# Attention turns of a hybrid mLSTM/Hyena layer: where the raw values are loaded, where the decay products are issued, and how the last two heads' outputs reach the next product

## The chip, the cores and the metric

One core of a Trainium2 chip runs the whole layer in one launch. The metric is the device time of the launch in microseconds; the number given for a kernel is the median of its runs. One more execution was taken with the hardware profiler, and every row below comes from it. Engines are named as in the profile: PE is TensorE (matmuls), PEld its weight loads, ACT is ScalarE, DVE is VectorE, POOL is GpSimd, SP is the engine whose queue issues most DMAs.

## What is computed

One trunk layer over 512 latent tokens of width 1024 with a context of 256 tokens: a modulated RMSNorm, two token mixers side by side (a bidirectional chunkwise mLSTM with 4 heads of width 256, and a Hyena long convolution), a gated merge of the two, an output projection, and a SwiGLU. Only the mLSTM part and what follows it matter here:

```
s   = einsum(q, k) * exp(logD - m_t)              # first products, times the decays
num = einsum(s, v) + a * einsum(C, q)             # second products
den = sum(s) + a * einsum(n, q)
h   = num / max(|den|, exp(-m_t))                 # per direction; h_f + h_b
hm  = head_norm(h_f + h_b, m_norm_g) * sigmoid(o)
y   = gm * (hm @ w_pm) + gh * (hh @ w_ph)         # hh: the Hyena branch
x   = x + g1 * (y @ w_out)
```

The kernel does it without a scan: for each head and direction it makes the full lower (or upper) triangle of decay factors, the context blocks included, so that one head is six source blocks of 128 tokens (four latent, two context) times four target blocks.

## The kernel before

Every fp32 product is made as three products of rounded halves (`mm3`: high times high, high times low, low times high), so each operand is split first: ACT writes the high half (L211), DVE subtracts for the low half (L212).

Raw data comes from DRAM through a ring of four buffers, tag `wr`. Through it go all weights (L236), the weight rows of the adaptive modulation (`wada`, L344, consumed by a DVE step at L354, one per call of `background`), and q, k and v of each head (L894). A buffer is given out in the order in which the program asks for buffers of the ring, and comes free when both halves of the split are made. Split weights go to `wh` and `wl`, four buffers each. The order of the work on each engine is laid down at compile time by a planner that follows the program's order, moves work marked with a high priority ahead, and keeps `behind()` work behind the last matmul of the latest tile product. Each engine then takes its list strictly in turn.

One head's turn, in the loop at L1336 to L1363:

- `load_head(h + 1)` (L885): q, k and v of the next head: five DMAs into the ring and their splits. q's halves have two buffers each, k's halves two buffers in all, v's halves (`vh`, `vl`) one each, so the split of v waits until the second products of the present head are done.
- `decay(h + 1, d)` (L851) for both directions: per direction four row products of 16 partitions into four of the `psH` banks (L862), one mask product (L864), and nine exponentials on ACT (L868).
- `values(h, 0)` (L930): the second products of direction 0, 54 matmuls over four target blocks; then `late`: `head_out` (L962) of the previous head: eight transposes (L966), gate and store of two tiles to DRAM (`hmd`, L976).
- `beside(h, 0)`: a tile of the Hyena projection `wph` (24 matmuls; in heads 0 to 2 only) and one `background` step.
- `weigh(h + 1)` (L913): the first products, 36 matmuls, each times the decays on DVE (L924). `values(h, 1)`; `halves(h + 1)`: the splits of the weighed decays (tags `dx`, `dy`); `beside(h, 1)`; `head_norm(h)` (L950: per target block statistics on DVE, one power on POOL, L958, one DVE step, L959).

In the last head there is no next head. After `late` it reloads six of the eight output tiles from `hmd` (L1265) and splits them; after the loop come two more `wph` tiles, the last `head_out`, whose two tiles are kept and split in SBUF, and the last `wph` tile. Then `staged_gemms("wpm", hm, ...)` makes the merge, whose `merge` calls `background` from its third tile on.

Of the kernel before, what the change touches and what calls it, by code (L numbers as in the profile page):

```python
# [8 lines left out]
F32 = mybir.dt.float32  # L9
# [10 lines left out]
NH = 4  # L20
# [136 lines left out]
def build(nc, tc, I, out, dbg=None):  # L157
# [18 lines left out]
    PR = [0]  # L176
# [5 lines left out]
    def T(p, shape, dt=F32, tag=None, bufs=None):  # L182
        uid[0] += 1
        p = HOME.get(tag, p)
        bufs = BUFS.get(tag, bufs)
        kw = {} if bufs is None else {"bufs": bufs}
        nm = f"{tag or 't'}_{uid[0]}"
        return p.tile(list(shape), dt, tag=tag or nm, name=nm, **kw)
# [21 lines left out]
    def split(hi, lo, x):  # L210
        act.activation(hi, x, AF.Copy)  # L211
        dve.tensor_sub(lo, x, hi.bitcast(F32))  # L212
# [640 lines left out]
    def decay(h, d):  # L853

        w = parts()
        rr = G["rr"]

        def rows(q, n, masked=False):
            ps = bank()
            g = slice(32 * q, 32 * q + 16)  # L860
            s_ = sel[g, 4 * d + h : 4 * d + h + 1].broadcast_to([16, 128])
            pe.matmul(ps[:, :n], s_, rr[g, :n], start=True, stop=not masked)  # L862
            if masked:
                pe.matmul(ps[:, :n], identr[:], mask[:, d : d + 1].broadcast_to([128, 4, 128]), start=False, stop=True)  # L864
            return ps

        def put(s, b0, n, ps, c0, bias):
            act.activation(  # L868
                piece(w, d, s)[:, b0 : b0 + n], ps[:, c0 : c0 + 128 * n].rearrange("p (a b) -> p a b", a=n), AF.Exp, bias=bias
            )  # L870

        pd = rows(0, 512, True)
        for s in range(4):
            put(s, 0 if d == 0 else PIECE[d][s][1] - 1, 1, pd, 128 * s, G["ad"][:, d, s, h : h + 1])
        pc = rows(1, 512)
        for s in range(2):
            put(4 + s, 0, 4, pc, 0, G["ax"][:, d, s, h : h + 1])
        p1 = rows(2, 384)
        p2 = rows(3, 384)
        o = [0, 1, 2] if d == 0 else [3, 2, 1]  # L880
        for s, ps, c0 in ((o[0], p1, 0), (o[1], p2, 0), (o[2], p2, 256)):
            put(s, 1 if d == 0 else 0, PIECE[d][s][1] - 1, ps, c0, G["ao"][:, d, s, h : h + 1])
        return w

    def load_head(h):  # L885

        kh, kl = (T(PT, [128, 2048], F32R, "K")[:, :1536].rearrange("p (a b) -> p a b", a=2) for _ in range(2))
        qh, ql = T(PT, [128, 2, SEQ], F32R, "uh"), T(PT, [128, 2, SEQ], F32R, "ul")

        def staged(src, n, hi, lo, a=None):  # L890
            t = T(PW, [128, WMAX], F32, "wr")[:, :n]
            if a:
                t = t.rearrange("p (a b) -> p a b", a=a)
            dma(t, src)  # L894
            split(hi, lo, t)

        staged(qd[:, 2 * h : 2 * h + 2], 2 * SEQ, qh[:], ql[:], 2)
        if h == 0:
            fill(next(cf))
        for i in range(2):  # L900
            staged(kd[:, 2 * h + i], SEQ + CTX, kh[:, i], kl[:, i])
        if h == 0:
            fill(next(cf))
        Vh, Vl = T(PM_, [128, 6, NV], F32R, "vh"), T(PM_, [128, 6, NV], F32R, "vl")
        gp.memset(Vh[:, :, 256:257].bitcast(F32), 1.0)
        gp.memset(Vh[:, :, 257:258].bitcast(F32), 0.0)
        gp.memset(Vl[:, :, 256:258].bitcast(F32), 0.0)
        for b, n in ((0, 4), (4, 2)):
            staged(vd[:, h, b : b + n], 256 * n, Vh[:, b : b + n, :256], Vl[:, b : b + n, :256], n)
        return (qh, ql), (kh, kl), (Vh, Vl)  # L910

    def weigh(h, qq, kk, Dm):

# [47 lines left out]
    def head_out(h, hs, keep=False):  # L961
        kept = []  # L962
        pt = [bank(), bank()]
        for t in range(4):
            for i in range(2):
                pe.transpose(pt[i][:, 128 * t : 128 * t + 128], hs[:, t, 128 * i : 128 * i + 128], ident)  # L966
        for i in range(2):
            hg = T(PM_, [128, 512], F32, "s2")
            act.activation(hg[:], pt[i][:], AF.Copy, scale=mngh[:, 2 * h + i : 2 * h + i + 1])
            o = T(PM_, [128, SEQ], F32, "s2")  # L970
            dma(o[:], od[:, 2 * h + i])
            dve.scalar_tensor_tensor(hg[:], o[:], 1.0, hg[:], op0=ALU.add, op1=ALU.mult)
            if keep:
                kept.append(hg)
            else:
                store(hmd[:, 2 * h + i], hg[:])  # L976
        return kept
# [166 lines left out]
    def background():  # L1144
        next(later, None)
# [39 lines left out]
    def fill(n):  # L1185
        for _ in range(n):
            if fills:
                fills.pop(0)()
# [98 lines left out]
            yield  # L1287

    fill(next(cf))
    heads = {0: load_head(0)}  # L1290
    sel = T(PM_, [128, 8], F32R, "sel")
    selr = load(PM_, "sel", [128, 8], "selr")
    act.activation(sel[:], selr[:], AF.Copy)
# [4 lines left out]
    act.activation(identr[:], ident, AF.Copy)  # L1298
    target_rows()

    def start(h):
        L = heads.get(h) or load_head(h)
        return L, [decay(h, d) for d in range(2)]

    def steps(n):
        for _ in range(n):
            background()

    L, Dm = start(0)
    fill(next(cf))  # L1310
    ada_row()
    weigh(0, L[0], L[1], Dm)
# [15 lines left out]
            next(ph)  # L1328
        steps(1)

    def late(_=None):
        if done:
            with behind():
                head_out(*done.pop())

    for h in range(NH):  # L1336
        nxt = start(h + 1) if h + 1 < NH else None
        den = T(PM_, [128, 2, 4], F32, "den", 2)
        hs = T(PM_, [128, 4, 256], F32, "hs", 2)
        values(h, 0, W[0], L[2], den, hs)  # L1340
        late(hs)
        if h == NH - 1:
            sp_ = [T(PT, [128, 2048], F32R, "K") for _ in range(2)]
            parts_ = [[v[:, 512 * j : 512 * j + 512] for j in range(4)] for v in sp_]
            for i, tag in enumerate(("uh", "ul")):
                v = T(PT, [128, 2, SEQ], F32R, tag)
                parts_[i] += [v[:, 0], v[:, 1]]
            its = [iter(v) for v in parts_]
            hm = reload(hmd, lambda: next(its[0]), lambda: next(its[1]), range(6))
        beside(h, 0)  # L1350
        if nxt:
            weigh(h + 1, nxt[0][0], nxt[0][1], nxt[1])
        values(h, 1, W[1], L[2], den, hs)
        if nxt:
            Wn = [halves(nxt[1][d]) for d in range(2)]
        beside(h, 1)
        head_norm(hs)
        done.append((h, hs))
        if nxt:
            L, W = nxt[0], Wn  # L1360
    next(ph)
    next(ph)
    with behind():  # L1363
# [45 lines left out]
    def merge(d, ps):  # L1409
        g = scr()  # L1410
        dma(g[:], gmd[:, 0, d])
        t = scr()
        dma(t[:], y2d[:, d])
        dve.scalar_tensor_tensor(g[:], g[:], 1.0, ps[:], op0=ALU.add, op1=ALU.mult)
        dve.tensor_add(g[:], g[:], t[:])
        y[0].append(big())
        y[1].append(big())
        split(y[0][-1][:], y[1][-1][:], g[:])
        if d > 1:
            background()  # L1420

    staged_gemms("wpm", hm, 3, 6, merge, KT)
    dve.tensor_scalar_mul(g1h[:], modT[:, 2, :, 0], 0.5)
# [146 lines left out]
```

## Time and profile before

| | |
|---|---|
| median of 3 runs | 1233.41 us (1231.26 to 1238.62) |
| the profiled execution's own time | 1238.27 us |
| its span in the trace | 1236.5 us |
| PE busy | 1196.6 us, 97% of the span |
| DVE, ACT, POOL busy | 835.0, 529.4, 68.2 us |
| mean granted clock of TensorE | 0.984 of full |

The span is the traced part of the execution; 1.8 us lie around it. Times in rows are microseconds from the span's start. The attention turns take the stretch from about 613 to 768 us. A busy PE may still be a slow one: the granted clock has two levels, 2.4 GHz (1.00) and 1.2 GHz (0.50), and a mean between them is a stretch that holds both.

### The profile page before, as it was taken

What the parts mean: (1) busy time and instruction counts of PE and PEld (TensorE: products, weight loads), DVE (VectorE), ACT (ScalarE), POOL (GpSimd) and SP (SyncE); (2) the same over time, 40 slices, a digit from 0 to 9 for tenths busy, and PEclk for the clock granted to TensorE, in tenths of its full rate; (3) what the DMA queues carried; (4) which work ended last, traced back from release to release, by engine and by line L of the source; (5) the groups of instructions that cost most, each with busy time, mean ns of one, the idle gap of its engine ahead of it and who ended that gap; (6) DMA issues with size and microseconds to landing.
All of it is one profiled execution on the core that took longest, in us unless ns stands there. A gap on an engine that the chain in (4) does not pass through costs nothing.

```text
span 1236.5 us, 16783 instructions
## 1 busy us (share of the span) xinstructions
PE 1196.6 (97%) x6440; PEld 1019.4 (82%) x6440; DVE 835.0 (68%) x1336; ACT 529.4 (43%) x824; POOL 68.2 (6%) x133
## 2 busy tenths in 40 slices
PE   4999999999999999999999988999999999999997
PEld 2799988888888888887788887889888888888886
DVE  6867798978989899796687776756653344332332
ACT  4754455654444544345664543323333223222321
POOL 0011110100010000101001111000000000000000
PEclk9899999999999999999998998999999999999998
DMA  9644452464343443336545647763443332333312
GB/s 355 231 167 149 158 179 86 162 221 137 103 131 116 147 135 128 120 117 227 188 143 173 219 153 244 244 230 119 136 140 100 102 94 94 98 91 97 94 47 69
DMA packets 61137, 183.78 MB, mean 149 GB/s; under 512 B 8440, under 2 KB 12288, under 8 KB 58880
## 3 DMA queue, kind: packets, MB, share of 16 engines
q1 hardware_dynamic: 53552, 153.86, 38.3%
q0 software_dynamic: 7504, 28.84, 6.3%
q8 instruction: 51, 0.84, 0.3%
q14 instruction: 30, 0.25, 0.1%
HBM read 151.74 MB, written 30.93 MB: 148 GB/s over the span
## 4 chain that ended last, share of the span: by engine, by line
PE 90%; DMA 5%; DVE 3%; ACT 1%; issue 1%; POOL 1%; SPq 0%; DVEq 0%; POOLq 0%; ACTq 0%
PE bank L215 27%; PE bank L216 26%; PE bank L217 26%; PE bank L641 2%; PE bank L643 2%; PE bank L642 2%; DMA wr<-in_wph 1%; PE bank L862 1%; PE bank L445 1%; PE bank L598 1%; DMA mats<-in_mats 1%; PE bank L446 1%; DMA hb<-in_dftf 1%; DMA hmd<-s 1%; DMA K<-in_wada 0%
## 5 line engine op out<-in xcount | busy, mean ns | idle before, releaser
L215 PE MATMUL bank<-hTh,wh 128*128 128x512 f32 (+1 forms) x952 | 368.3, 389 | 2.5 <-ACT hTh L1070 2.0
L216 PE MATMUL bank<-hTl,wh 128*128 128x512 f32 (+1 forms) x952 | 367.6, 387 | 2.2 <-DVE hTl L1076 2.2
L217 PE MATMUL bank<-hTh,wl 128*128 128x512 f32 (+1 forms) x952 | 367.0, 386 | 0.0
L211 ACT ACTIVATE wh<-wr 128x1024 fp32r<-128x1024 f32 (+1 forms) x167 | 172.3, 1033 | 434.5 <-PE bank L216 215.5
L212 DVE TENSOR_TENSOR wl<-wr,wh 128x1024 fp32r<-128x1024 f32 (+1 forms) x167 | 198.1, 1189 | 177.6 <-ACT wh L211 176.4
L215 PEld LDWEIGHTS bank<-hTh,wh 128*128 128x128 f32 x952 | 179.8, 189 | 38.0 <-ACT hTh L1070 2.2
L216 PEld LDWEIGHTS bank<-hTl,wh 128*128 128x128 f32 x952 | 179.8, 189 | 37.2 <-DVE hTl L1076 2.5
L217 PEld LDWEIGHTS bank<-hTh,wl 128*128 128x128 f32 x952 | 179.8, 189 | 35.3
L216 PE MATMUL bank<-big,wh 128*128 128x512 f32 (+1 forms) x266 | 95.3, 358 | 0.0
L217 PE MATMUL bank<-big,wl 128*128 128x512 f32 (+1 forms) x266 | 95.0, 357 | 0.0
L215 PE MATMUL bank<-big,wh 128*128 128x512 f32 (+1 forms) x266 | 95.0, 357 | 0.0
L354 DVE SCALAR_TENSOR_TENSOR wr<-wr,crow 128x1024 f32<-128x1024 f32 x32 | 39.0, 1222 | 26.3 <-DMA wr<-in_wada 26.2
L216 PEld LDWEIGHTS bank<-big,wh 128*128 128x128 f32 x266 | 50.8, 191 | 7.2
L215 PEld LDWEIGHTS bank<-big,wh 128*128 128x128 f32 x266 | 50.8, 191 | 7.1
L217 PEld LDWEIGHTS bank<-big,wl 128*128 128x128 f32 x266 | 50.8, 191 | 7.0
L211 ACT ACTIVATE hb<-hb 128x512 fp32r<-128x512 f32 (+1 forms) x49 | 36.7, 768 | 28.5 <-DVE hb L450 18.1
L1514 DVE TENSOR_TENSOR s<-s,bank 128x512 f32<-128x512 f32 x22 | 15.1, 686 | 46.4 <-PE bank L217 46.4
L212 DVE TENSOR_TENSOR hb<-hb,hb 128x512 fp32r<-128x512 f32 (+1 forms) x49 | 40.4, 864 | 2.0 <-ACT hb L211 1.8
L641 PE MATMUL bank<-wh,hTh 128*128 128x256 f32 (+1 forms) x128 | 36.4, 285 | 0.0
L643 PE MATMUL bank<-wh,hTl 128*128 128x256 f32 (+1 forms) x128 | 36.4, 284 | 0.0
L642 PE MATMUL bank<-wl,hTh 128*128 128x256 f32 (+1 forms) x128 | 36.4, 284 | 0.0
L373 POOL TENSOR_TENSOR rr<-rv,negh 128x2 f32<-128x2 f32 (+1 forms) x6 | 5.5, 924 | 514.3 <-DVE rv L371 514.3
(376 smaller groups left out, 2200.8 us busy)
## 6 DMA issues: line engine op xcount, KB each, us to landing
wr<-in_win SPq DMA_DIRECT2D x64, 512.0 KB, 3.7
wr<-in_w SPq DMA_DIRECT2D x60, 512.0 KB, 3.7
wr<-in_wada SPq DMA_DIRECT2D x32, 512.0 KB, 4.7
Kd<-K POOLq DMA_DIRECT2D x8, 1024.0 KB, 4.5
K<-Kd SPq DMA_DIRECT2D x8, 1024.0 KB, 5.7
wr<-in_wv SPq DMA_DIRECT2D x8, 512.0 KB
gmd<-s POOLq DMA_DIRECT2D x16, 256.0 KB, 2.6
wr<-in_wph SPq DMA_DIRECT2D x8, 512.0 KB, 4.4
```

The lines of the kernel that those rows point to most:

```text
L211: act.activation(hi, x, AF.Copy)
L212: dve.tensor_sub(lo, x, hi.bitcast(F32))
L215: pe.matmul(o, wh, xh, start=first, stop=False)
L216: pe.matmul(o, wh, xl, start=False, stop=False)
L217: return pe.matmul(o, wl, xh, start=False, stop=last)
L354: dve.scalar_tensor_tensor(w, w, 1.0, crow[:], op0=ALU.mult, op1=ALU.mult, accum_out=s)
L445: pe.matmul(ps[:], lhs, w4h, start=True, stop=False)
L446: pe.matmul(ps[:], lhs, w4l, start=False, stop=True)
L641: pe.matmul(o, xh, wh, start=bool(k == 0), stop=False)
L642: pe.matmul(o, xh, wl, start=False, stop=False)
L643: m = pe.matmul(o, xl, wh, start=False, stop=bool(k == KT - 1))
L1514: dve.tensor_tensor(t[:], t[:], pb[:], op=ALU.mult)
```

## The change

The loads are cut in two. `load_head` loads and splits q and k alone; a new `load_values(h)` makes and fills `vh` and `vl`. Inside the loop, for heads 0 to 2, `load_values(h + 1)` now stands behind `values(h, 1)`. The first direction's decays of the next head stand ahead of `values(h, 0)`, behind the last matmul before it, and the second direction's stand behind `values(h, 0)`. In the last head the first four output tiles are reloaded, ahead of `values(3, 0)`; the previous head's `head_out` comes behind `values(3, 1)` and keeps its two tiles, which are split in SBUF; `head_norm(3)` has a high priority; and the two `background` steps of this head are gone. `merge` calls `background` for all of its eight tiles.

```diff
+    def staged(src, n, hi, lo, a=None):
+        t = T(PW, [128, WMAX], F32, "wr")[:, :n]
+        if a:
+            t = t.rearrange("p (a b) -> p a b", a=a)
+        dma(t, src)
+        split(hi, lo, t)
+
     def load_head(h):
...
         staged(qd[:, 2 * h : 2 * h + 2], 2 * SEQ, qh[:], ql[:], 2)
         if h == 0:
             fill(next(cf))
         for i in range(2):
             staged(kd[:, 2 * h + i], SEQ + CTX, kh[:, i], kl[:, i])
-        if h == 0:
-            fill(next(cf))
+        return (qh, ql), (kh, kl)
+
+    def load_values(h):
         Vh, Vl = T(PM_, [128, 6, NV], F32R, "vh"), T(PM_, [128, 6, NV], F32R, "vl")
         gp.memset(Vh[:, :, 256:257].bitcast(F32), 1.0)
         gp.memset(Vh[:, :, 257:258].bitcast(F32), 0.0)
         gp.memset(Vl[:, :, 256:258].bitcast(F32), 0.0)
         for b, n in ((0, 4), (4, 2)):
             staged(vd[:, h, b : b + n], 256 * n, Vh[:, b : b + n, :256], Vl[:, b : b + n, :256], n)
-        return (qh, ql), (kh, kl), (Vh, Vl)
+        return Vh, Vl
...
-    heads = {0: load_head(0)}
+    L = load_head(0)
+    fill(next(cf))
+    V = load_values(0)
...
-    L, Dm = start(0)
+    Dm = [decay(0, d) for d in range(2)]
...
-    def late(_=None):
+    def late(keep=False):
         if done:
             with behind():
-                head_out(*done.pop())
-
+                ends.extend(head_out(*done.pop(), keep))
+
+    ends = []
     for h in range(NH):
-        nxt = start(h + 1) if h + 1 < NH else None
+        last = h == NH - 1
...
-        values(h, 0, W[0], L[2], den, hs)
-        late(hs)
-        if h == NH - 1:
+        if last:
...
-            hm = reload(hmd, lambda: next(its[0]), lambda: next(its[1]), range(6))
-        beside(h, 0)
-        if nxt:
-            weigh(h + 1, nxt[0][0], nxt[0][1], nxt[1])
-        values(h, 1, W[1], L[2], den, hs)
-        if nxt:
-            Wn = [halves(nxt[1][d]) for d in range(2)]
-        beside(h, 1)
-        head_norm(hs)
+            hm = reload(hmd, lambda: next(its[0]), lambda: next(its[1]), range(4))
+        else:
+            L = load_head(h + 1)
+            with behind():
+                D0 = decay(h + 1, 0)
+        values(h, 0, W[0], V, den, hs)
+        if not last:
+            with behind():
+                Dm = D0, decay(h + 1, 1)
+            late()
+            beside(h, 0)
+            weigh(h + 1, L[0], L[1], Dm)
+        values(h, 1, W[1], V, den, hs)
+        if last:
+            late(True)
+        else:
+            V = load_values(h + 1)
+            W = [halves(Dm[d]) for d in range(2)]
+            beside(h, 1)
+        with tc.high_priority(PR[0] if last else 0):
+            head_norm(hs)
         done.append((h, hs))
-        if nxt:
-            L, W = nxt[0], Wn
+    for t in ends:
+        for i in range(2):
+            hm[i].append(next(its[i]))
+        split(hm[0][-1], hm[1][-1], t[:])
     next(ph)
     next(ph)
...
         split(y[0][-1][:], y[1][-1][:], g[:])
-        if d > 1:
-            background()
+        background()
```

## Rows read from the trace of the kernel before

**Rows 1.** Engine totals of the page: busy us, share, instructions.

```profile
PE 1196.6 (97%) x6440; PEld 1019.4 (82%) x6440; DVE 835.0 (68%) x1336; ACT 529.4 (43%) x824; POOL 68.2 (6%) x133
```

**Rows 2.** Busy time by stage; columns: length, PE, PEld, DVE, ACT, POOL, granted clock, DMA.

```profile
644.00:660.10 16.10, 15.03 (x66) 11.98 (x66) 10.79 (x30) 9.76 (x25) 3.25 (x7) 0.68 0.49 153
...
697.20:716.40 19.20, 16.71 (x74) 13.54 (x73) 12.84 (x28) 7.02 (x11) 1.66 (x3) 0.91 0.79 259
...
728.10:744.00 15.90, 14.17 (x118) 13.86 (x117) 11.10 (x39) 6.08 (x16) 4.81 (x7) 1.00 0.71 234
744.00:768.00 24.00, 20.04 (x82) 15.96 (x82) 15.63 (x41) 7.48 (x12) 3.35 (x6) 0.86 0.65 219
...
784.30:815.00 30.70, 30.70 (x137) 25.40 (x136) 27.17 (x40) 10.62 (x14) 0.00 (x0) 1.00 0.90 302
```

**Rows 3.** Busy time in two five-microsecond stretches, same columns.

```profile
580.00:585.00 5.00, 4.99 (x28) 3.36 (x26) 3.74 (x6) 3.65 (x6) 0.54 (x1) 1.00 0.98 336
...
755.00:760.00 5.00, 1.04 (x6) 0.49 (x4) 3.15 (x10) 0.86 (x1) 1.99 (x4) 0.74 0.37 122
```

**Rows 4.** Timeline where values(0, 1) ends and values(1, 0) begins; bracket: idle before.

```profile
644.17 1.58 ACT L211 ACTIVATE vh<-wr 128x1024 fp32r<-128x1024 f32 x2 [0.97 <-PE bank L217]
...
645.34 1.83 DVE L212 TENSOR_TENSOR vl<-wr,vh 128x1024 fp32r<-128x1024 f32 x2
...
644.01 0.50 PE L862 MATMUL bank<-rrow,sel 16*128 16x512 f32 x1
644.43 0.50 PE L864 MATMUL bank<-mask,identr 128*128 128x512 f32 x1
...
645.85 0.59 PE L215 MATMUL bank<-vh,dx 128*128 128x258 f32 x3 [0.49 <-issue]
647.01 0.49 PE L862 MATMUL bank<-rrow,sel 16*128 16x512 f32 x1 [0.57 <-ACT dx L868]
```

**Rows 5.** The decays' exponentials (L868): count, ns min/median/max, first and last start.

```profile
L868 ACT ACTIVATE dy<-bank,ad x32: 351/388/451, 589.9 to 692.4; 128x128 f32<-128x128 f32 x32
L868 ACT ACTIVATE dy<-bank,ao x24: 360/502/692, 586.3 to 695.7; 128x384 f32<-128x384 f32 x8, 128x256 f32<-128x256 f32 x8, 128x128 f32<-128x128 f32 x8
L868 ACT ACTIVATE dx<-bank,ax x16: 672/705/787, 585.1 to 694.3; 128x512 f32<-128x512 f32 x16
```

**Rows 6.** Timeline of ACT after values(1, 0): copies out of the banks, gate copy.

```profile
660.31 1.56 ACT L946 ACTIVATE hs<-bank,den 128x256 f32<-128x256 f32 x4
661.74 0.71 ACT L969 ACTIVATE s<-bank,mngh 128x512 f32<-128x512 f32 x1
```

**Rows 7.** Timeline of SP: the loads of head 1's v.

```profile
591.49 6.89 SPq L894 DMA_DIRECT2D wr<-vd  x2
```

**Rows 8.** Waits of SP's queue, 600 to 790 us: total us, times, longest.

```profile
SPq L236 <- DVE vl L212: 21.4, 3, 10.4
```

**Rows 9.** Timeline of ACT, DVE and PE in weigh(3).

```profile
710.46 1.06 ACT L211 ACTIVATE wh<-wr 128x1024 fp32r<-128x1024 f32 x1 [4.06 <-DMA wr<-in_wph]
...
711.55 1.23 DVE L212 TENSOR_TENSOR wl<-wr,wh 128x1024 fp32r<-128x1024 f32 x1 [2.65 <-ACT wh L211]
...
713.53 0.76 PE L215 MATMUL bank<-uh,K 128*128 128x512 f32 x1 [2.49 <-DVE dx L924]
```

**Rows 10.** Timeline of the last two heads' norms and outputs.

```profile
733.92 0.54 POOL L958 TENSOR_TENSOR rs<-rs,negh 128x1 f32<-128x1 f32 x1 [0.66 <-DVE den L944]
735.12 1.51 POOL L958 TENSOR_TENSOR rs<-rs,negh 128x1 f32<-128x1 f32 x1 [0.66 <-DVE den L944]
...
735.02 1.21 DVE L354 SCALAR_TENSOR_TENSOR wr<-wr,crow 128x1024 f32<-128x1024 f32 x1
...
737.13 0.44 PE L966 MATMUL bank<-mats,hs 128*128 128x128 f32 x2 [1.73 <-DVE hs L959]
...
752.83 0.63 ACT L211 ACTIVATE uh<-s 128x512 fp32r<-128x512 f32 x1 [1.72 <-DMA s<-hmd]
...
759.61 0.69 PE L966 MATMUL bank<-mats,hs 128*128 128x128 f32 x2 [3.34 <-DVE hs L959]
```

More of the change, by code (lines that the diff above doesn't have):

```diff
@@ L888, in load_head @@
         qh, ql = T(PT, [128, 2, SEQ], F32R, "uh"), T(PT, [128, 2, SEQ], F32R, "ul")
[L890 to L895, printed above, removed]
         staged(qd[:, 2 * h : 2 * h + 2], 2 * SEQ, qh[:], ql[:], 2)
@@ L1299, in build @@
     target_rows()
-    def start(h):
-        L = heads.get(h) or load_head(h)
-        return L, [decay(h, d) for d in range(2)]
     def steps(n):
```

## The prediction

> **What bounds the kernel now.** I read the engine totals first: PE is busy 97% of the span [rows 1], so the time is the sum of PE's work plus what PE loses. The change alters no matmul, so only the losses can change. Busy time by stage shows them: PE idles, or works at the lower of its two clock levels, in four stages between 613 and 768 us [rows 2]. For each stage the loss is length minus busy time, plus (1 - granted clock) x length, less what would be counted twice (idle time at the low clock).
>
> - **A**, 644 to 660 (decays of head 2, second products of head 1): idle 1.07, clock 0.32 x 16.1 = 5.15, together 6.2 us.
> - **B**, 697 to 716 (first products for head 3): idle 2.49, clock 0.09 x 19.2 = 1.73, of which some 0.25 was idle: 4.0.
> - **C**, 728 to 744: idle 1.73 at full clock: 1.7.
> - **D**, 744 to 768: idle 3.96, clock 0.14 x 24 = 3.36; of it 1.15 fell on idle time (in 755 to 760 PE is busy for 1.04 at a mean clock of 0.74, so about 2.3 us of idle passed at half clock [rows 3]): 6.2.
>
> Together **18.1 us**. That is the most that the change can win. Then I read the timelines around each loss for the instruction that released PE.
>
> **Part 1: the raw values.** v of head 1 is asked for from 591.5 us on [rows 7], but its split can only start once `values(0, 1)` has ended (644.17 [rows 4]). So two of the ring's four buffers stood full for some 50 us, and the next weights queued behind them: SP waited three times for the low half of v before it could ask for weights, 21.4 us in all, 10.4 the longest [rows 8]. This is where B comes from: a `wph` load came so late that ACT's split stood 4.06 us and DVE's 2.65 us behind it, and the decay steps queued on DVE behind that split kept `weigh(3)` off its banks: PE idle 2.49 us [rows 9]. In the changed program the order of requests in a head is q, k, k, `wph`, `wada`, v, v, `wph`, `wada`. Both v loads have moved past one weight load and one `wada` load on SP, and two `wada` loads of the last head have left for the merge. Buffers are given as they come free, so v will still arrive ahead of its need; I cost it at nothing, the cover being the weights and products of half a turn. If the cover is gone, `values(h + 1, 0)` waits for a load, two splits and what DVE has queued; rival 3 prices it. I take B's 4.0 as won, with 0 and 4.0 as bounds, since a weight that lands late in another place would cost the same.
>
> **Part 2: the decays in two sets.** Before, both sets (10 small products, 18 exponentials) were issued between the second products. One set is on ACT 4 x 0.388 + 3 x 0.502 + 2 x 0.705 = 4.5 us [rows 5], and four banks hold one set; so PE, strictly in turn, stood for a bank (0.57 on the exponential, 0.49 before [rows 4]), and in A the clock fell with it. Now one set stands ahead: five products at 0.43 us start to start [rows 4] = 2.15, from 644.0 to 646.2. The split of v is the same as before: high halves till 644.17 + 1.58 = 645.75, low halves till 645.34 + 1.83 = 647.17 [rows 4]. The first products of `values(1, 0)` need both, so PE still idles 0.9 us here. In heads 2 and 3 a `wph` tile, 24 products at 30.70 / 137 = 0.224 = 5.4 us [rows 2], covers the split. Whether the clock falls again can't be read off the idle time alone: 1.06 us of idle in A cost 5.15, 1.73 in C cost nothing [rows 2, 10]. Bounds are 0 and 5.15; I take 1.5, the fall after B's idle, because there as here undivided large products follow. A's remainder: 2.4 (0.9 to 6.1).
>
> A set alone does not slow PE: from 580 to 585 it ran 14 transposes and the first small products at clock 1.00 [rows 3].
>
> The second set is the added wait. `weigh(h + 1)` needs it, and on PE the following lie between: the set 2.15, `head_out` (8 transposes at some 0.12) 1.0, one `wph` tile 5.4; 8.5 us in all. On ACT the exponentials follow the first small product by its 0.5 and take 4.5, so 3.5 are left. Other work that may come first is four copies out of the banks 1.56, two gate copies 2 x 0.71 [rows 6] and one weight split 1.06 [rows 9], 4.0 in all: at worst 0.5 short in each of three heads. I put 0.5 for the three together, 0 to 1.5. Queued behind a late exponential on ACT are weight splits, and PE waits for those as well.
>
> **Part 3: the last two heads.** C: the transposes of head 2 stood behind `values(3, 0)` and waited for its norm [rows 10]. Now they stand behind `values(3, 1)`, 54 products x 0.12 (14.17 / 118 [rows 2]) = 6.5 us later; C goes: 0 left, bound 0.5.
>
> D: the norm of head 3 stood in DVE's list behind the split of a reloaded tile, whose data went to DRAM and back and reached ACT at 752.83 [rows 10]; PE waited until 759.61. Two stores and two reloads now fall away, and the norm has priority. Its cover between `values(3, 1)` and its own transposes is 1.0 + 2 x 5.4 = 11.8 us. It needs four rounds of about 1.2 (0.54 on POOL [rows 10] and the DVE steps), 5 us. POOL's power took 1.51 instead of 0.54 beside a `wada` step on DVE [rows 10], which makes 6 us. The Trainium skill, SBUF — State Buffer, section "Who interferes with whom", says that a DVE instruction with two SBUF inputs contends with a GpSimd instruction that reads SBUF, and the kept tiles' splits are such instructions, now placed right beside this norm; the row agrees, and by the rule all four rounds could be slowed, 5 + 4 x 0.97 = 9 us. Both are under 11.8.
>
> D goes; if DVE also stood 2.65 as in B it would be used up, so I keep 0 to 1.0.
>
> The two `background` steps moved into the merge add 2 x 1.3 us to DVE, which has 27.17 of 30.70 us there while PE never idles [rows 2]: 0, bound 2.6. Their two loads join a stretch where the DMA engines are 0.90 busy [rows 2]; the weights are asked for well ahead, so 0.
>
> For waits that no row shows, a DMA that lands later than planned in a new order, I add 1.0 (0 to 4.0, another B).
>
> **Sum.** Left over: 2.4 + 0.5 + 1.0 = 3.9, so 14.2 of 18.1 us are won: 1238.27 - 14.2 = 1224.1 for an execution like the profiled one. That one lies 4.9 above the median. If the excess sits in these stalls, the median after is 1224.1; if elsewhere, 1233.41 - 14.2 = 1219.2. No row decides; I take the middle, **1221.5 us**.
>
> **Rivals.**
> 1. *The move moves nothing.* Buffers are given as they come free, so v may be fetched as early as before, and weights still come late. For: two weight loads earlier in a long list is little. Against: the loads now ahead of v are the very ones that waited. B stays (4.0): 1225.5.
> 2. *The second set comes too late* (slower). If ACT stands for a weight's DMA ahead of those exponentials, as it did 4.06 us [rows 9], the margin of 3.5 us is gone and `weigh` waits in three heads, each with idle and a fall of the clock as in A: 3 x 6.2 = 18.6, against 14.2 + 0.5: 1233.4 + 3.9 = 1237.3. It decides from the point at which what ACT does or waits for ahead of them passes 3.5 us. Against: half of the other work isn't needed early, and weights now come sooner.
> 3. *v comes too late.* If its load starts only as `values(h, 1)` ends, a landing of some 5 us goes ahead of the split; exposed only in head 1, the others having a tile as cover: 5 and a fall of the clock as in A, say 8: 1229.5.
>
> **How the numbers follow.** Forecast 0.62 (1215.5 to 1226), rival 1 0.22 (1222 to 1229), rival 2 0.08, rival 3 0.08 (1226 to 1233). The range 1215.5 to 1231 leaves out rival 2 and half of rival 3; its lower end is the whole 18.1 us. About 1% (12.3 us) is what a measurement of this kernel can tell from no change; faster by more means under 1221.1. Half to two thirds of the forecast and a little of rival 1 lie there: 0.44. Slower by 1% would need rival 2 and more: 0.03. The rest, 0.53, is within 1%.
>
> **What would show it.** No `wph` load waits for the low half of v; in `weigh(3)` DVE has no split standing for a weight. Five small products, then undivided second products, with under 1 us of idle where head 1 begins. The transposes of heads 2 and 3 without idle, no reload of more than four tiles. Wrong would be: PE idle on L924 or L868 in `weigh` (rival 2), on a split of v (rival 3), or granted clocks of 0.5 in a stretch that was at 1.00.

## The result and the profile after

The changed kernel takes **1228.6 us** (median of 19 runs, 1226.2 to 1230.75) against 1233.43 for the kernel before (19 runs, 1230.08 to 1241.24, same chip): ratio **0.995**, 95% interval 0.9936 to 0.9964. It is faster, by 4.8 us in the medians and 6.2 in the means (1234.76 to 1228.60). Forecast was 1221.5, within 1215.5 to 1231.0. The direction and the range held; of the 14.2 us that the sum promised, between a third and under a half came.

Engine totals of the page, which answer to [rows 1]. The span is 1228.9 us, the execution's own time 1230.75:

```profile
PE 1189.2 (97%) x6440; PEld 1014.0 (83%) x6440; DVE 834.1 (68%) x1336; ACT 528.3 (43%) x824; POOL 69.1 (6%) x131
```

Busy time by stage after the change, columns as in [rows 2] (length, PE, PEld, DVE, ACT, POOL, granted clock, DMA). The first row is the whole attention stretch, from the first small product of head 1's decays to the merge's first product. The others are E1, a wait named below, and what follows it, the start of head 1 (A), `weigh(3)` (B), the middle and the end of the last head (C, D), and the merge:

```profile
613.65:762.42 148.77, 138.82 (x795) 118.94 (x795) 109.58 (x264) 76.53 (x159) 19.96 (x37) 0.97 0.54 174
...
627.00:634.00 7.00, 4.73 (x14) 3.44 (x13) 3.20 (x4) 3.96 (x8) 0.44 (x1) 0.76 0.19 47
642.80:658.00 15.20, 12.63 (x75) 11.52 (x75) 14.43 (x39) 9.71 (x23) 3.00 (x7) 0.78 0.50 157
698.40:716.40 18.00, 16.83 (x85) 13.60 (x83) 12.96 (x25) 9.46 (x18) 1.68 (x4) 1.00 0.73 233
736.50:745.40 8.90, 7.83 (x65) 7.70 (x65) 7.29 (x29) 2.65 (x10) 2.60 (x3) 1.00 0.37 120
745.00:762.60 17.60, 17.60 (x84) 14.67 (x83) 12.49 (x33) 5.71 (x8) 3.60 (x5) 1.00 0.62 210
779.00:809.70 30.70, 30.70 (x137) 25.44 (x136) 26.73 (x38) 10.02 (x13) 0.00 (x0) 1.00 0.86 292
```

The same stretch of the kernel before, by the same view:

```profile
613.19:767.79 154.60, 145.36 (x796) 123.11 (x796) 114.62 (x270) 78.18 (x162) 19.07 (x39) 0.93 0.56 184
```

So 5.8 us of the stretch are gone. (The two profiled executions lie 7.5 us apart, 1238.27 and 1230.75. The rest is some 2.2 us in the last 135 us of the launch, far behind the change, less 0.5 ahead of the stretch; and the one before lies 4.8 above its median.) Read against [rows 2]: C and D are clean (745.00 to 762.60 is PE without a gap at clock 1.00; the 1.07 in the row ahead of it is a new wait, E5 below), and the merge still has none, with two more background steps in it. But PE idles for 148.77 - 138.82 = 9.95 us, as much as before (9.24). The idle time has moved. PE's timeline after the change, the rows with a wait and the set of decay products that stands where head 1 begins:

```profile
629.54 0.50 PE L215 MATMUL bank<-hTh,wh 128*128 128x512 f32 x1 [2.27 <-ACT hTh L211]
...
647.44 0.50 PE L862 MATMUL bank<-rrow,sel 16*128 16x512 f32 x1
647.87 0.50 PE L864 MATMUL bank<-mask,identr 128*128 128x512 f32 x1
648.30 0.49 PE L862 MATMUL bank<-rrow,sel 16*128 16x512 f32 x3
649.29 0.48 PE L215 MATMUL bank<-vh,dx 128*128 128x258 f32 x2 [0.50 <-issue]
651.84 0.58 PE L216 MATMUL bank<-vl,dx 128*128 128x258 f32 x1 [2.07 <-DVE vl L212]
...
700.59 0.66 PE L967 MATMUL bank<-mats,hs 128*128 128x128 f32 x4 [1.16 <-ACT dy L868]
...
724.35 0.47 PE L215 MATMUL bank<-hTh,wh 128*128 128x512 f32 x1 [2.87 <-DVE den L945]
...
737.66 0.39 PE L215 MATMUL bank<-vh,dx 128*128 128x258 f32 x1 [1.07 <-ACT hs L947]
```

I name these waits **E1** (627 us, a `wph` tile), **A** (649, head 1's second products), **E3** (699, the transposes of head 1's output), **E4** (721, the fifth `wph` tile), **E5** (737, the last second products). `weigh(3)` has no wait (B is gone), the transposes of heads 2 and 3 have none (C and D are gone).

ACT's timeline shows what E1 and E4 stand behind:

```profile
624.70 0.63 ACT L211 ACTIVATE hTh<-s 128x512 fp32r<-128x512 f32 x1 [0.93 <-DMA s<-hhd]
625.24 1.12 ACT L868 ACTIVATE dy<-bank,ad 128x128 f32<-128x128 f32 x4
...
626.59 1.29 ACT L868 ACTIVATE dx<-bank,ax 128x512 f32<-128x512 f32 x2
627.73 1.25 ACT L868 ACTIVATE dy<-bank,ao 128x384 f32<-128x384 f32 x3
628.79 1.22 ACT L211 ACTIVATE hTh<-s 128x512 fp32r<-128x512 f32 x2
...
716.40 0.64 ACT L211 ACTIVATE K<-s 128x512 fp32r<-128x512 f32 x1 [2.73 <-DMA s<-hmd]
717.79 0.63 ACT L211 ACTIVATE K<-s 128x512 fp32r<-128x512 f32 x1 [0.76 <-DMA s<-hmd]
719.63 0.63 ACT L211 ACTIVATE K<-s 128x512 fp32r<-128x512 f32 x1 [1.21 <-DMA s<-hmd]
720.17 1.26 ACT L211 ACTIVATE dy<-dy 128x1280 fp32r<-128x1280 f32 x1
721.33 0.15 ACT L943 ACTIVATE den<-bank 128x1 f32<-128x1 f32 x1
```

In E1 the exponentials of the second set stand between the splits of the reloaded rows of `hhd`; PE needs the last two of these rows, split from 628.79. In E4 the denominator of head 2, which DVE needs before it can empty the bank that PE waits for, stands behind three splits that wait for reloaded tiles of `hmd`, 4.7 us in all. DVE's timeline, for A and for E4:

```profile
647.45 1.21 DVE L212 TENSOR_TENSOR dx<-dx,dx 128x1024 fp32r<-128x1024 f32 x1
648.57 1.22 DVE L212 TENSOR_TENSOR wl<-wr,wh 128x1024 fp32r<-128x1024 f32 x1
649.71 0.22 DVE L944 TENSOR_TENSOR den<-den,em 128x1 f32<-128x1 f32 x2
649.85 1.22 DVE L212 TENSOR_TENSOR vl<-wr,vh 128x1024 fp32r<-128x1024 f32 x1
...
721.51 0.16 DVE L944 TENSOR_TENSOR den<-den,em 128x1 f32<-128x1 f32 x1 [4.02 <-ACT den L943]
```

The split of v's low halves starts 2.3 us after the second products end (647.51), behind two other splits; before it started 1.3 us after they ended (644.08; 645.34 in [rows 4]). SP's timeline, answering to [rows 7], and its waits from 600 to 790 us, answering to [rows 8]:

```profile
600.86 9.87 SPq L889 DMA_DIRECT2D wr<-vd  x2
...
612.74 10.29 SPq L1266 DMA_DIRECT2D s<-hhd  x8
```

```profile
SPq L236 <- DVE vl L212: 10.5, 3, 9.9
```

v is asked for 9.4 us later than before, just ahead of the reload of `hhd`, and the weights' wait for its low half has halved, from 21.4 to 10.5.

### The profile page after: what moved, and what is told of

Read it like the earlier page. It is cut to its first block, busy times and chain, and to the rows that moved or that the text cites. A ratio compares the mean times of both kernels' runs of the same rounds, so it can differ in the third digit from the quotient of the medians.

```text
span 1228.9 us, 16765 instructions
## 1 busy us (share of the span) xinstructions
PE 1189.2 (97%) x6440; PEld 1014.0 (83%) x6440; DVE 834.1 (68%) x1336; ACT 528.3 (43%) x824; POOL 69.1 (6%) x131
## 4 chain that ended last, share of the span: by engine, by line
PE 88%; DVE 5%; DMA 3%; issue 2%; ACT 2%; POOL 0%; SPq 0%; DVEq 0%; POOLq 0%; ACTq 0%
PE bank L215 26%; PE bank L216 26%; PE bank L217 25%; PE bank L641 2%; PE bank L642 2%; PE bank L643 2%; DMA s<-hhd 1%; DMA wr<-in_wph 1%; PE bank L445 1%; PE bank L598 1%; PE bank L446 1%; DMA hmd<-s 1%; PE bank L319 1%; DVE wl L212 1%; DMA ul<-in_xT 0%
```

## The experiments

Each ratio is to the kernel before in the same session, with its 95% interval. Session medians of the kernel before were 1234.52 (the first four kernels below), 1232.61 (those of E1, the old rows, and the first two with the moved tile) and 1235.54 (the other four), so ratios are what compares across sessions; the changed kernel's is 0.995. They are the ratios on record and differ by up to 0.0014 from the quotient of the two medians, so differences of 0.1% between sessions mean nothing.

### The parts one by one

The first four kernels and two later ones leave out parts of the change, so that with both kernels every combination is there. Theory N: new waits made by the changed order eat the gain; theory L: only the last two heads matter.

**Last two heads alone.** The changed kernel with v asked for behind q and k, and both sets ahead of the second products:

```diff
-            L = load_head(h + 1)
-            with behind():
-                D0 = decay(h + 1, 0)
+            L, Vn = load_head(h + 1), load_values(h + 1)
+            Dm = [decay(h + 1, d) for d in range(2)]
...
-            with behind():
-                Dm = D0, decay(h + 1, 1)
...
-            V = load_values(h + 1)
+            V = Vn
```

> The kernel before with the last two heads' part alone (v loaded and both decay sets issued as before). Theory N (new waits eat the gain): the waits C 1.7 and D 6.2 go, and the two waits that the changed kernel shows in the last two heads come in their place, 2.9 where a weight tile waits for banks behind the reload's splits and 1.1 ahead of the last second products; A (6.2) stays; of B (4.0) up to half goes, two loads having left the queue. 1233.4 - 3.9 - (0 to 2) = 1227.5 to 1229.5. Theory L (only the last two heads matter, the other two parts do nothing): the time of the changed kernel, 1228.6, within 1.

Measured: 1225.67 us (1220.64 to 1230.8, 7 runs), ratio **0.9922** (0.9894 to 0.995), faster than both theories said.

**Without the two sets.** Of these edits, only those on the sets:

```diff
-            with behind():
-                D0 = decay(h + 1, 0)
+            Dm = [decay(h + 1, d) for d in range(2)]
...
-            with behind():
-                Dm = D0, decay(h + 1, 1)
```

> The changed kernel with both decay sets issued ahead of the first second products again; v's late load and the last heads' part stay. Theory N: the wait of the first weight tile for its operands behind the second set's exponentials (2.3 idle and some 1.8 of low clock) and the wait of transposes for a bank (1.2) go; the sets cost PE some 1.1 more per head, three times, because they are cut up among the second products again: 1228.6 - 5.3 + 3.4 = 1226.7, and no PE wait on a set in weigh. Theory L: 1228.6 within 1.

Measured: 1226.95 us, ratio **0.9934** (0.9909 to 0.9959): theory N's time, though the interval overlaps that of the whole change.

**Without the later load of v.**

```diff
-            L = load_head(h + 1)
+            L, Vn = load_head(h + 1), load_values(h + 1)
...
-            V = load_values(h + 1)
+            V = Vn
```

> The changed kernel with v asked for right behind q and k again; the two sets and the last heads' part stay. Theory N: weights queue behind v again, so a late weight split returns in one of the turns (0 to 4.0), while no weight split stands ahead of v's own split where head 1 begins (2.6 idle there falls to about 1): 1228.6 - 1.6 to + 4 = 1227 to 1232.6. Theory L: 1228.6 within 1.

Measured: 1232.99 us, ratio **0.9989** (0.9975 to 1.0003): just above the upper end of theory N. The late weight is back (2.25 us in `weigh(3)`).

**Without the last two heads' part.** The last heads' outputs, reload (six tiles), norm (without priority) and background steps as in the kernel before; the cut leaves out lines that only move:

```diff
-            hm = reload(hmd, lambda: next(its[0]), lambda: next(its[1]), range(4))
+            hm = reload(hmd, lambda: next(its[0]), lambda: next(its[1]), range(6))
...
-            late()
...
+        late()
...
-        if last:
-            late(True)
-        else:
+        if not last:
...
-        background()
+        if d > 1:
+            background()
```

> The changed kernel with the last two heads as before: reload of six tiles behind the first second products, outputs through DRAM, the two steps in the last head. Theory N: C 1.7 and D 6.2 return, the two new waits of the last heads (2.9 and 1.1) go: 1228.6 + 3.9 = 1232.5, B's loss staying away. Theory L: all the gain lies in the last heads, so the time of the kernel before, 1233.4, within 1, and B's loss of 4.0 back in the third turn.

Measured: 1234.91 us, ratio **1.0** (0.9984 to 1.0016): the time that theory L gave. E1 is there, 2.28 us, and 1.12 us of a wait in `weigh(3)`.

**The later load of v alone** (that kernel, with both sets ahead of the second products):

```diff
-            with behind():
-                D0 = decay(h + 1, 0)
+            Dm = [decay(h + 1, d) for d in range(2)]
...
-            with behind():
-                Dm = D0, decay(h + 1, 1)
```

> The kernel before with the part on the raw values alone: both sets ahead of the second products, the last two heads as they were. Theory B (what the prediction said of this part): the 2.5 us of idle time and 1.7 of low clock in the first products of head 3 go, 1233.0 - 4.0 = 1229. Rival L (the gain of the whole lies in the last two heads; the loads' place does nothing by itself, since another wait takes the place of that one): 1232 to 1235.

Measured: 1233.51 us, ratio **0.9984** (0.9969 to 0.9999): rival L. The wait in `weigh(3)` did go (2.49 to 0.26 us), but other waits grew: 0.62 us ahead of head 3's transposes became 2.26.

**The two sets alone** (that kernel, with v asked for behind q and k):

```diff
-            L = load_head(h + 1)
+            L, Vn = load_head(h + 1), load_values(h + 1)
...
-            V = load_values(h + 1)
+            V = Vn
```

> The kernel before with the part on the two sets alone, the raw values asked for behind q and k. Theory N (the second set's exponentials come late on ScalarE and hold up the tile of wph of head 0 and later steps, and one set covers the split of v less than two did): idle time of 2 us or more at 627 us and near 647 us, 4 to 7 us more than before: 1237 to 1240. Rival L (the sets do nothing of themselves): 1232 to 1235.

Measured: 1231.37 us, ratio **0.9971** (0.9958 to 0.9985). Both theories missed: it is faster. The wait at 647 us is there (0.78 and 1.54), the one at 627 us is not.

All together, in one table. Stretch, PE busy and idle are of the one profiled execution of each (first small product of head 1's decays to the merge's first product). The clock's share is PE busy less 137.3, or less 134.9 where the sets are cut in two: what PE takes at full clock, from two profiles of each kind that had none or next to none of the low clock (137.52 and 137.05; 134.88 in the run with sets and the moved tile, below); it is an estimate, good to some 0.3 us. One execution need not be the median: the profiled one of the kernel before lies 4.8 us above its median, that of the last heads' part 5.0 below.

| parts in | ratio | stretch | idle | clock |
|---|---|---|---|---|
| none (before) | 1 | 154.60 | 9.24 | 8.1 |
| v | 0.9984 | 149.68 | 8.05 | 4.3 |
| sets | 0.9971 | 147.95 | 8.19 | 4.9 |
| v, sets | 1.0 | 153.40 | 12.76 | 5.7 |
| last heads | 0.9922 | 140.41 | 2.89 | 0.2 |
| last heads, v | 0.9934 | 142.86 | 4.35 | 1.2 |
| last heads, sets | 0.9989 | 151.41 | 12.13 | 4.4 |
| all (after) | 0.995 | 148.77 | 9.95 | 3.9 |

Theory L holds in one half: the last heads' part alone measures more than the whole, 0.78% or 9.6 us against 0.5% (the intervals overlap). It fails in the other, since the other two parts don't do nothing. With the last heads' part in, the sets cost 0.67% without the later v (0.9922 to 0.9989) and the later v gives 0.39% back once the sets are there (0.9989 to 0.995); in both pairs the intervals lie apart. The parts don't add up. The last heads' part gives 0.78% alone, 0.50% beside the later v, 0.50% beside both and -0.18% beside the sets alone; the later v gives between 0.39 and -0.29%, the sets between 0.29 and -0.67%.

### What makes E1

```diff
-        hh = reload(hhd, slots("hTh"), slots("hTl"))
+        with tc.high_priority(PR[0]): hh = reload(hhd, slots("hTh"), slots("hTl"))
```

> The changed kernel with priority for the reload of the rows that the first tile of wph needs, so that ScalarE splits them ahead of the exponentials of the second set. Theory N (the second set's exponentials, standing between those splits on ScalarE, hold up the tile): the wait of 2.3 us at 627 us goes and with it some 1.7 us of low clock, 1228.6 - 4 = 1224.6. Rival R (ScalarE has no room there: what goes ahead only pushes the exponentials back): the first products of head 1 wait for their bank or for DVE instead, by 2 us or more, and the time stays at 1227 to 1229.5.

Measured: 1225.21 us (1223.36 to 1226.57), ratio **0.9926** (0.9905 to 0.9947), 0.24% under the change; the intervals overlap, but the trace shows the wait gone and no low clock behind it. Theory N holds. PE's timeline in place of the 2.27 us, with the first products of head 1 at the end:

```profile
622.93 0.50 PE L215 MATMUL bank<-hTh,wh 128*128 128x512 f32 x1 [0.31 <-ACT hs L947]
...
628.41 0.50 PE L216 MATMUL bank<-hTl,wh 128*128 128x512 f32 x1 [0.19 <-DVE hTl L212]
...
630.73 0.50 PE L215 MATMUL bank<-uh,K 128*128 128x512 f32 x1 [0.19 <-ACT dx L868]
```

The exponentials could wait: `weigh(1)` lost 0.19. And E1 needs two parts at once: it is in the profiles with the sets and the later v, with and without the last heads' part (2.27 and 2.28 us), and in none of those without one of the two. With the sets alone ACT's list is in the same order, but the reload was asked for at 610.27 instead of 612.74 and the second set's exponentials began at 622.43 instead of 625.24. The two v loads, moved on SP to just ahead of the reload, made the difference.

### What makes E4

First, the last reload reads tiles that are long in DRAM (so the merge gets other rows as input, and the output is another one):

```diff
-            hm = reload(hmd, lambda: next(its[0]), lambda: next(its[1]), range(4))
+            hm = reload(hhd, lambda: next(its[0]), lambda: next(its[1]), range(4))
```

> The changed kernel with the last reload reading four tiles of hhd, long in DRAM, in place of the four of hmd, which are stored just ahead of it; the output is another one, the instructions and their order are the same. Theory N (ScalarE's list stands at a split that waits for a store and a reload, with the denominator of head 2 queued behind it): the 2.9 us wait of the fifth tile of wph at 721 us goes down to under 0.7, ScalarE doesn't wait for these loads, 1228.6 - 2.4 = 1226.2. Rival S (the denominator would come late anyway, behind DVE's sums and the splits of the weights): the wait stays over 2 us and the time at 1228 to 1229.

Measured: 1228.96 us, ratio 0.9961 (0.9946 to 0.9977); the wait stays, 2.60 us. That looks like rival S, but the edit didn't take the cause away. SP's waits, 695 to 722 us:

```profile
SPq L1266 <- DMA hmd<-s: 5.6, 2, 4.8
```

The loads no longer read `hmd` and still wait 5.6 us for its stores: they go into the scratch tiles that the stores read from. ACT stood 4.4 us for the loads, 4.7 in the change. So the run tells nothing of N or S. The next one takes the splits out of ACT's way:

```diff
-            hm = reload(hmd, lambda: next(its[0]), lambda: next(its[1]), range(4))
...
             late(True)
+            hm = reload(hmd, lambda: next(its[0]), lambda: next(its[1]), range(4))
```

> The changed kernel with the last reload (four tiles of hmd, split on ScalarE and DVE) taken from ahead of the last head's products to behind its output, so that ScalarE's list no longer has these splits ahead of the denominators of head 2; the rest of that list is the same. Theory N (ScalarE's list stands at these splits for loads that come late, and the denominator is queued behind): the wait of 2.9 us of the fifth tile of wph at 721 to 724 us goes, 1228.6 - 2.9 = 1225.7. Rival S (the denominator would be late anyway, or the splits now stand ahead of the norm of head 3 or of the merge): a wait of 2 us or more at 721 us or at 745 to 760 us, and 1228 to 1230.

Measured: 1225.22 us (1224.08 to 1226.39), ratio **0.9924** (0.9903 to 0.9944), 0.26% under the change (overlapping at the ends): N, and almost to the number. ACT's timeline around the denominator, and the stretch:

```profile
714.14 1.28 ACT L211 ACTIVATE dy<-dy 128x1280 fp32r<-128x1280 f32 x1 [2.18 <-DVE dy L925]
715.44 0.17 ACT L943 ACTIVATE den<-bank 128x1 f32<-128x1 f32 x1
```

```profile
612.12:756.25 144.13, 137.87 (x795) 118.47 (x795) 111.94 (x266) 77.07 (x160) 19.20 (x37) 0.96 0.55 181
```

The denominator is copied at 715.44, before the second products are even over; E4 is gone, and E5 with it (idle 6.26 us, 3.7 less). The edit takes the splits' low halves off DVE's list too, so how much of E4 was ACT's and how much DVE's isn't separated.

### Cover where head 1 begins

Head 0's `wph` tile goes from behind its first to behind its second products, so that PE has 24 products there while v is split. Three kernels have this one edit: the last heads' part alone, the whole change, and the change without the sets.

```diff
-    PHN = ((1, 0), (1, 1), (1, 1), (0, 0))
+    PHN = ((0, 1), (1, 1), (1, 1), (0, 0))
```

**With the last heads' part alone.**

> The part on the last two heads alone, with the tile of wph of head 0 moved from behind the first to behind the second products of the first direction pair, so that it covers the split of v where head 1 begins. Theory P (PE stands where head 1 begins only for lack of products between the end of the second products and the split of the new values): the 1.06 us of idle time that the part alone has at 645 to 647 us go, and with them the fall of the clock that some executions show there; 1225.7 - 1.1 = 1224.6 if only the idle time counts, about 1221 if the clock fell in most executions. Rival Q (the tile is missed as much where it stood): idle time of 1 us or more appears ahead of the first products of head 1, at 618 to 630 us, and the time stays at 1225 to 1226.

Measured: 1226.02 us (1225.38 to 1227.55), ratio 0.9937 (0.9918 to 0.9956): no gain over 0.9922. The wait where head 1 begins did go (0.46 us for the tile's weight is left), but neither theory foresaw the rest: 2.39 us in `weigh(3)` and 2.59 ahead of the last second products, both with a low clock behind them. ACT's timeline names the first:

```profile
704.04 1.06 ACT L211 ACTIVATE wh<-wr 128x1024 fp32r<-128x1024 f32 x1 [8.12 <-DMA wr<-in_wph]
```

It is loss B again: a weight that lands late, with a split standing for it.

**With the whole change.**

> The changed kernel with the same tile of wph moved in the same way. Theory P: the 2.6 us of idle time where head 1 begins and the 2.6 us lost to the clock behind it go; what waits at 627 us for the reloaded rows goes as well, since the tile runs 15 us later, but the first products of head 1 then stand directly behind the second set and wait for its exponentials, some 3 us with perhaps 2 of clock: 1228.6 - 5.2 - 4 + 5 = 1224.4. Rival Q (the second set of exponentials needs a tile as cover more than the split does): the wait ahead of the first products of head 1 is over 5 us and the time is 1227 to 1231.

Measured: **1222.36 us** (1221.5 to 1222.79), ratio **0.9904** (0.9885 to 0.9923), 5.7 us under the change (0.46% of 1233). P holds, and the wait for the second set's exponentials that it reckoned with, 3 us and 2 of clock, isn't there at all, so the time is 2 us better than P's. The stretch and what is left of PE's waits over 0.3 us:

```profile
613.68:753.57 139.89, 134.88 (x795) 115.12 (x795) 110.75 (x265) 78.00 (x160) 21.19 (x37) 1.00 0.55 185
```

```profile
703.96 0.47 PE L215 MATMUL bank<-uh,K 128*128 128x512 f32 x1 [0.97 <-DVE dx L925]
707.74 0.47 PE L215 MATMUL bank<-uh,K 128*128 128x512 f32 x1 [1.07 <-DVE dx L925]
728.80 0.39 PE L215 MATMUL bank<-vh,dx 128*128 128x258 f32 x1 [2.25 <-ACT hs L947]
```

The second of them is of B's kind again, though v is asked for late here: DVE's step stands behind a weight's split, and ACT's timeline has that weight late.

```profile
704.08 1.06 ACT L211 ACTIVATE wh<-wr 128x1024 fp32r<-128x1024 f32 x1 [4.19 <-DMA wr<-in_wph]
```

**Without the sets.**

> The changed kernel without the two sets (both ahead of the second products) and with the tile of wph of head 0 moved behind the second products, as in the run that gave 1222.4. Theory P (with that tile in place the sets cost nothing any more and let PE begin the second products earlier): 1225 to 1227, slower than 1222.4 by 2 us or more, the waits of 2 to 2.6 us in the first products of head 3 and ahead of its second products of the second direction pair standing as in the other kernel with both sets ahead and this tile moved. Rival Q (the sets still cost what they did, some 2 to 7 us): 1216 to 1220.

Measured: **1221.28 us** (1219.85 to 1223.04), ratio **0.9891** (0.9871 to 0.991). Both theories missed: P said that it would be slower than the run with the sets, Q that it would be faster still, and the 0.13% between the two is inside the intervals. The sets neither pay nor cost once that tile is in place: their undivided products save PE 2.4 us (137.3 to 134.9), and idle time gives it back (2.87 here, 5.01 there). Beside the first of the three, only the later v differs, and the weight in `weigh(3)` comes in time:

```profile
698.83 1.06 ACT L211 ACTIVATE wh<-wr 128x1024 fp32r<-128x1024 f32 x1 [2.03 <-DMA wr<-in_wph]
```

PE doesn't wait there, and the later v is worth 0.46% (0.9937 to 0.9891, the intervals don't overlap).

These last two kernels are faster than both kernels of the case, the second by some 13 us against the kernel before.

## Why the prediction was right in direction and off in size

**"The change alters no matmul, so only losses can change."** Half right. The products are the same, but PE's time for them is not: a set that is not cut up by second products takes 1.35 us (647.44 to 648.79), as the last three row products share one span of 0.49, where I took five starts at 0.43, 2.15 us. The first set of the kernel before shows the same, in a row that follows those of [rows 4]:

```profile
644.87 0.49 PE L862 MATMUL bank<-rrow,sel 16*128 16x512 f32 x3
```

Only its second set was cut up. Keeping that whole gives PE 2.4 us over the stretch, and the shorter set also takes 0.8 us off the cover of v's split in A.

**Part 1, v (4.0 us won).** The mechanism of B is right, and B is gone after the change. In every pair of profiles that differ in this part alone and show a late `weigh(3)`, the wait shrinks: 2.49 to 0.26 without the other parts, 0.94 to none with the last heads' part, 2.25 to none with that and the sets, 2.39 to none with the moved tile. (With the sets alone there was none, and the later v brought 1.12; with the moved tile and all parts 1.07 stands behind a late weight.) The 4.0 did not come whole: alone the part measures 0.16%, 2 us, and other waits grew. And what it was costed at, nothing, fell: I named the queue past which the loads move, but reckoned only with v's own arrival, not with what stands behind v now. That is the reload of `hhd`, and E1 is the bill.

**Part 2, the sets (0.5 us for the second set).** This is the step that failed first. The second set's exponentials are late on ACT as rival 2 said, but not in `weigh`: E1 takes 2.27 us and some 1.7 for the low clock behind it (0.24 of the 7.00 us from 627), E3 1.16, where a transpose waits for a bank that the set holds. 5.1 us against 0.5, with a bound of 1.5. I had counted how long `weigh` can wait for the exponentials. That splits queue behind them and PE waits for those too I did say, of weights, but it got no term; the splits that came late were those of the rows of `hhd`, which PE needs before `weigh`.

**A's remainder (2.4 us, 0.9 to 6.1).** Idle 2.57, and the clock at 0.50 from 651.84 to 657.8, where starts lie 0.21 us apart instead of 0.12. Up to half of that is lost, 3.0: together 5.6 at most, in the bounds and over the value taken. The shorter set makes 0.8 of it and the two splits ahead of v's low half on DVE 1.2. That a tile as cover removes it is shown by the three runs with the moved tile.

**Part 3, the last two heads (C and D, 7.9 us).** Right in place and size: C and D are gone, and alone the part measures 9.6 us (6.2 to 13), with 1.55 us of B's wait among them (2.49 to 0.94). The norm of head 3 runs from 742.36 to 752.15 and is done 3.9 us ahead of its transposes at 756.08. That is 9.8 us from its first step and 7.7 from the end of the second products (744.44), near the estimate of 5 to 9. One of POOL's four powers was slowed, 1.39 us against 0.54 for the others, and it is the one beside a `wada` step on DVE, of which both inputs lie in SBUF:

```profile
749.12 0.54 POOL L959 TENSOR_TENSOR rs<-rs,negh 128x1 f32<-128x1 f32 x1 [1.83 <-DVE rs L958]
750.32 1.39 POOL L959 TENSOR_TENSOR rs<-rs,negh 128x1 f32<-128x1 f32 x1 [0.65 <-DVE rs L958]
```

```profile
750.09 1.21 DVE L354 SCALAR_TENSOR_TENSOR wr<-wr,crow 128x1024 f32<-128x1024 f32 x1
```

The rule that the prediction cites, the Trainium skill, SBUF — State Buffer, section "Who interferes with whom", agrees with that power. Beside the other three DVE ran no such instruction, and the kept tiles' splits came only behind the norm, so the trace doesn't test it there. The background steps cost nothing in the merge, as said.

**"Waits that no row shows" (1.0, 0 to 4.0).** E4 and E5 are 3.9 us, at the upper bound. E4's stores of `hmd` are behind the weights' splits on DVE, the reload behind the stores, ACT's list behind the reload; with the last heads' part alone, the tiles were there and ACT did not stand. The run that moved the reload shows it.

**The sum.** Left over were to be 3.9 us; 9.95 + 3.9 = 13.9 are left. Against that stand the 2.4 that PE's work fell: 17.3 - 13.9 + 2.4 = 5.8, the change of the stretch. The time fell in the range because the range was wide: of the parts only the last two heads' gave what the sum took from them, the losses that came back were partly met by work on PE that the sum did not have, and 1228.6 lies among the times given to rival 1, which is not what happened. That much is luck. Rival 2 came true in one head, for other instructions than it named. Rival 3's wait came too, though not from the load, which was asked for 47 us ahead. Rival 1 has a trace in SP's waits: I expected no weight to wait for the low half of v, and 10.5 of 21.4 us still do. I had priced the rivals as whole outcomes, while pieces of them belonged in the sum.

What stays open: why the sets without the later v cost as much as they do beside the last heads' part (12.13 us idle, of which 3.89 in E4's place and 2.78 in E5's) and gain alone, and what makes E5. In the profile of the sets beside the last heads' part ACT again stands at the splits of `hmd`, 5.1 us in all, with two denominators between and behind them. The list of waits names places, and no run took them apart.

## What to carry to other kernels

When a load is moved past others in a queue, cost what now stands behind it as well as its own arrival. An engine that works strictly in turn makes everything behind a waiting split late, so ask of each instruction placed in its list who needs the ones after it first, and keep a block of independent products where a single-buffered operand is re-split. Parts of one change do not add up: measured apart and together, the later load of v gained 0.46% in one setting (0.9937 to 0.9891) and lost 0.29% in another (0.9971 to 1.0, the intervals just touching).

## What the runs showed of the hardware

**The same idle time did or did not bring the low clock.** In the kernel before 1.06 us of idle at 645 to 647 us were followed by some 10 us at 0.50 (the 0.68 over 16.1 us in [rows 2]). With the last heads' part alone the same wait is there, and the clock stays at its upper level:

```profile
645.00:650.00 5.00, 4.12 (x21) 2.96 (x22) 4.56 (x11) 4.83 (x15) 1.11 (x2) 1.00 0.59 200
650.00:655.00 5.00, 5.00 (x41) 4.68 (x39) 3.97 (x11) 3.31 (x10) 1.94 (x3) 1.00 0.20 57
```

That kernel's seven runs range over 10 us, 1220.64 at a mean clock of 0.996 to 1230.8 at 0.986; the two kernels with all three of part 3, the later v and the moved tile, which have no idle time there, range over 1.3 and 3.2 us. 2.25 us of idle in one of them, at 728 us, left the clock at 1.00. So one profile can't price such a wait: of these two, one lost its idle time and the other several microseconds more. For the executions that weren't profiled only the mean clock is known, so that they differ in this place is not shown.

**Three row products in one span.** The rows at 648.30 above are three products from 16 partitions each, recorded together with 0.49 us. In the kernel before, among second products, those of the second set have starts of their own (649.53, 650.98 and 652.75).
